# First token block of a hybrid decoder layer: scaling after the projections, and identity transposes on TensorE

## The chip, the cores and the metric

One core of a Trainium2 chip runs the whole layer in one program. The metric is the device time in microseconds of one execution. A profiled execution gives the trace that the rows below are read from.

## What is computed

A decoder layer on 2048 tokens of width 1024: a mixer (a gated linear recurrence beside a convolution module), attention into 256 fixed memory tokens, a convolutional gated feed-forward part, a last normalization. The change touches the first normalization and the projections that follow it:

```python
h = rms_norm(x, mix_norm_g)              # x * rsqrt(mean(x*x) + eps) * g, per token
z = h @ w_in                             # 1024 -> 2048
lru_x, lru_gate, conf_a, conf_b = jnp.split(z, [512, 1024, 1536], axis=-1)
lru_x = causal_dwconv(lru_x, lru_conv_w) + lru_conv_b
y_lru = rg_lru(lru_x, ...) * gelu(lru_gate)
c = causal_dwconv(conf_a * sigmoid(conf_b), conf_conv_w) + conf_conv_b
```

The factor rsqrt(mean(x*x) + eps) belongs to a token, so that multiplying a token by it before `h @ w_in` or the token's results after it is the same thing.

## The kernel before

**Order of the work.** The body of the program doesn't issue instructions. Generators (`mixer`, `memory_a`, `normed`, `attend`, `memory_vo`, `feed_forward` and others) append operations to a list, each stepping when a running count of TensorE work reaches its due time; of the due ones the first in the list `tasks` steps. A planner (`Program.schedule`) then plays all operations through with estimated costs, and so fixes the order in which each engine, and SP's queue of loads and stores, gets them. It ranks ready operations by due times derived from TensorE's order, except those appended while `pr.first` is set: they are ranked by their place in the list, ahead of all others. Buffers of a kind (84 of class S with 512 columns, 4 of class W for raw weights, 3 of class D for convolution inputs, 8 banks `ps`) are granted in the order in which the list asks for them. On the chip each engine keeps its planned order and waits on semaphores. Because every operation is emitted by the planner, the profile puts them all at L393; the names of the tiles tell them apart.

**Precision.** Operands are split into a rounded high part and the rest (`split`: a copy on ACT, a subtraction on VectorE; `split_scaled` does it with a factor for each channel). A product is three matmuls (`mm3`) of 128 by 128 against 128 by 512.

**Query block 0.** Tokens come in four blocks of 512, `q` = 0 to 3. `mixer(0)` starts with `first_norm` (from line 1055 of before): it loads the 8 tiles of x, then the first two raw blocks of w_in (`W_in.fetch`, columns 1536 to 1791, rows 0 to 511 and 512 to 1023), sums squares on ACT, turns the tokens on TensorE (8 times 4 transposes of 128 by 128) and multiplies by the gains, gets the token factors (square root, reciprocal), spreads them over all partitions by a matmul of `ones` and four diagonal matrices, multiplies the turned tokens by that row, splits them and multiplies: 8 steps `k` of 2 times 3 matmuls, 48 for one project of 256 columns. Before them `setup` has loaded the four gains (`v1024`), which TensorE turns as well.

**After it.** `conf` runs for c = 0 and 2: a project for the sigmoid (the first one is the one above), a project for its partner, product `cb`, 31 taps of convolution on VectorE (30 `scalar_tensor_tensor` a channel block into `conv`). `lru` runs for c = 0 and 2: project z, four taps that read the bank of z directly (`xc`), the last three columns of z kept in `ztail`, then gates, the recurrence, and a project with Gelu. In `memory_a`, beside it, the memory's keys and `w_q` are multiplied (tiles `kv`, `qt`, `mt`, `a`). Blocks q = 1 to 3 take `mix_norm` instead, which scales the tokens before it turns them. After a mixer, `normed` sums the convolutions (`sum`) for a layer norm, and `attend` goes on.

Of the kernel before, what the change touches and what calls it, by code (L numbers as in the profile page):

```python
# [14 lines left out]
ALU = mybir.AluOpType  # L15
# [19 lines left out]
LK = 4  # L35
# [381 lines left out]
def hybrid_layer(  # L417
# [336 lines left out]
    W_in = Columns(w_in[0], "w_in2", 16, NQ)  # L754
    W_out = Rows(w_out[0], "w_out2", 8, NQ)

    def conf(X, C, pb):
        for c in (0, 2):
            if pb is None:
                pb = yield from project(W_in, 3 * DL + c * P, X)  # L760
            sg = []
            for j in range(2):
                t = tmp("sg")
                ACT(t[:], pb[j][:], AF.Sigmoid)
                sg.append(t)
            pb = None
            yield 0
            pa = yield from project(W_in, 2 * DL + c * P, X)
            cbs = []
            for j in range(2):  # L770
                cb = pr.new("D", (P, CK - 1 + TT), name="cb")
                V("tensor_copy", cb[:, : CK - 1], ctail[c + j][:])
                V("tensor_tensor", cb[:, CK - 1 :], pa[j][:], sg[j][:], op=ALU.mult)
                V("tensor_copy", ctail[c + j][:], cb[:, TT : TT + CK - 1])
                cbs.append(cb)
            for j in range(2):
                a, cb, w = tmp("conv"), cbs[j], vec["v512"][:, c + j, :]
# [19 lines left out]

    def conf_out(C, Y):
        s = block_sum(C, False)
        yield 2  # L800
        p = ps()
        matmul(p[:], ones[:], s[:], start=True, stop=True)
        for c in range(NC4):
            V("tensor_tensor", C[c][:], C[c][:], p[:], op=ALU.subtract)
        ss = block_sum(C, True)
        yield 6
        r = wide_rstd(ss, 1.0)
        for c in range(NC4):
            w = vec["v512"][:, c, :]
            V("scalar_tensor_tensor", C[c][:], C[c][:], w[:, I_LG : I_LG + 1], r[:], op0=ALU.mult, op1=ALU.mult)  # L810
            ACT(C[c][:], C[c][:], AF.Silu, bias=w[:, I_LB : I_LB + 1])
            hi, lo = pair("y")
            split(C[c][:], hi, lo)
            Y.append((hi, lo))

    def lru(X, L):
        for c in (0, 2):
            pz = yield from project(W_in, c * P, X)
            H = []
            for j in range(2):  # L820
                w = vec["v512"][:, c + j, :]
                zt = ztail[c + j]
                xc = tmp("xc")
                ACT(xc[:], pz[j][:], AF.Identity, scale=w[:, I_LCW + 3 : I_LCW + 4], bias=w[:, I_LCB : I_LCB + 1])
                for s in range(1, LK):
                    wt = w[:, I_LCW + 3 - s : I_LCW + 4 - s]
                    V("scalar_tensor_tensor", xc[:, s:], pz[j][:, : TT - s], wt, xc[:, s:], op0=ALU.mult, op1=ALU.add)
                    V("scalar_tensor_tensor", xc[:, :s], zt[:, LK - 1 - s :], wt, xc[:, :s], op0=ALU.mult, op1=ALU.add)
                V("tensor_copy", zt[:], pz[j][:, TT - LK + 1 :])
                H.append(xc)  # L830
            yield 5
            for j in range(2):
                w = vec["v512"][:, c + j, :]
                xc = H[j]
# [25 lines left out]
            pg = yield from project(W_in, DL + c * P, X)  # L860
            for j in range(2):
                ge = tmp("gelu")
                ACT(ge[:], pg[j][:], AF.Gelu_apprx_tanh)
                V("tensor_tensor", ge[:], H[j][:], ge[:], op=ALU.mult)
                hi, lo = pair("y")
                split(ge[:], hi, lo)
                L.append((hi, lo))
# [32 lines left out]
    def memory_a():  # L900
# [30 lines left out]
        yield 2  # L931
        def operands(h):
            kk = yield from kv(h * M)
            yield 0
# [36 lines left out]

    def memory_vo():
        yield mem_a
        for h in range(4):
            vh, vl = yield from kv(D + h * M)
            yield 1
# [65 lines left out]
    def mixer(q, after):  # L1042
        if after:
            yield after
        if q == 0:
            X, pb = yield from first_norm()
        else:
            X, pb = (yield from mix_norm(q)), None
        C, L = [], []
        yield from conf(X, C, pb)  # L1050
        yield from lru(X, L)
        del X
        mixed[q] = C, L

    def first_norm():


        pr.first = True
        warm = small(1)
        ACT(warm[:], eps[:], AF.Sqrt)  # L1060
        xs = [[None, None] for _ in range(NTB)]
        st, T = Stats(), []
        for half in range(2):
            for tb in range(NTB):
                t = xs[tb][half] = tmp("x")
                pr.dma(t[:], x[0, tb * P : (tb + 1) * P, half * TT : (half + 1) * TT])
        raw = [W_in.fetch(3 * DL, kq) for kq in range(2)]
        for half in range(2):
            for tb in range(NTB):
                st.add(tb, half, xs[tb][half][:])  # L1070
            for k in range(half * KQ, (half + 1) * KQ):
                p = ps()
                with together():
                    for tb in range(NTB):
                        transpose(p[:, tb * P : (tb + 1) * P], xs[tb][half][:, (k % 4) * P : (k % 4 + 1) * P], ident[:])
                if not half:
                    t = tmp("xt")
                    V("tensor_scalar", t[:], p[:], vec["v1024"][:, k, G_MIX : G_MIX + 1], None, op0=ALU.mult)
                    p = t
                T.append(p)  # L1080
        del xs
        r = st.rstd()
        p, diag = ps(), []
        for tb in range(NTB):

            d = pr.new("S", (P, P), name="diag")
# [5 lines left out]
        ww = [W_in.rounded(3 * DL, 0, raw[0])]  # L1092
        X, pp = [], [ps(), ps()]
        for k, t in enumerate(T):
            if k < KQ:
                V("tensor_tensor", t[:], t[:], p[:], op=ALU.mult)
            else:
                if k == KQ:
                    row = tmp("row")
                    ACT(row[:], p[:], AF.Copy)  # L1100
                z, t = t, tmp("xt")
                V("scalar_tensor_tensor", t[:], z[:], vec["v1024"][:, k, G_MIX : G_MIX + 1], row[:], op0=ALU.mult, op1=ALU.mult)
            hi, lo = pair("x")
            split(t[:], hi, lo)
            X.append((hi, lo))
            if k == 1:
                ww.append(W_in.rounded(3 * DL, 1, raw[1]))
            kq, i = divmod(k, KQ)
            for f in range(2):
                wh, wl = ww[kq][f]  # L1110
                with together():
                    mm3(pp[f][:], wh[:, i, :], wl[:, i, :], hi[:], lo[:], k == 0, k == NK - 1)
        W_in.store(3 * DL, 0, ww[0])
        W_in.store(3 * DL, 1, ww[1])
        pr.first = False
        yield 0
        return X, pp

    def mix_norm(q):
        xs = load_x(q, "x")  # L1120
# [8 lines left out]
        yield 8  # L1129
        X = []  # L1130

        def take(k, p):
# [16 lines left out]
    def attend(q, ready):  # L1149
# [17 lines left out]
        yield 2  # L1167
        X = []

        def take(k, p):  # L1170
# [34 lines left out]
                row.append(t)  # L1205
            ys.append(row)
        del xs
        yield 6

        def take2(k, p):  # L1210
            t = tmp("xt")
# [341 lines left out]
        yield V_LATE  # L1553
        vec["v3072"] = columns([ffn_conv_w[0], ffn_conv_b], DFF, "v3072")

    EARLY, VO_WAIT, V_LATE = 5, 0, 500
    X = [HalfX(h) for h in range(NH)]

    def first_x():
        yield first_t  # L1560
        yield started[NQ - 1]
        for key in UP_ORDER[:EARLY]:
            X[0].make(key)
            yield 20

    def feed_forward():
        yield first
# [13 lines left out]
            tasks.insert(0, Task(finish(h, downs[h].acc)))  # L1581

    setup()
    mixers = [None] * NQ
    attends = [None] * NQ
    mixers[0] = spawn(mixer(0, None))
    spawn(setup_later(), mixers[0])
    mem_a = spawn(memory_a())
    mixers[1] = spawn(mixer(1, mixers[0]))
    normeds = [None] * NQ  # L1590
    normeds[0] = spawn(normed(0, [mixers[0]], 40))
    attends[0] = spawn(attend(0, [normeds[0]]))
    mem_vo = spawn(memory_vo())
    mixers[2] = spawn(mixer(2, mixers[1]))
    normeds[1] = spawn(normed(1, [attended[0]], 90), mixers[2])
    attends[1] = spawn(attend(1, [normeds[1]]))
    mixers[3] = spawn(mixer(3, mixers[2]))
    normeds[2] = spawn(normed(2, [attended[1]], 90), mixers[3])
    normeds[3] = spawn(normed(3, [mixers[3], normeds[2]], 55))
    attends[2] = spawn(attend(2, [normeds[2]]))  # L1600
    attends[3] = spawn(attend(3, [normeds[3], attended[2]]))
    first_t = spawn(X[0].kept(normeds[3], 10), attends[2])
    first = spawn(first_x(), attends[2])
    tail = spawn(feed_forward())
    drive()
    pr.emit(tc)

# [30 lines left out]
```

## Time and profile before

| | us |
|---|---|
| median of 3 runs | 2511.07 |
| lowest and highest | 2508.03, 2512.06 |
| profiled execution, device time | 2507.09 |
| its span, first to last instruction | 2505.3 |
| its mean granted TensorE clock | 0.996 |

Busy in the span: TensorE 2463.5 us, its weight loads 2037.9, VectorE 1820.2, ACT 1166.4, GpSimd 0.7. The DMA engines moved 543.68 MB, 217 GB/s on the mean.

In rows of the trace, PE is TensorE, PEld its weight loads, DVE VectorE, SPq the queue that issues transfers. A row of the view in order of time has the start, the time from the first start to the last end, the engine, the source line, the operation, `out<-in`, the shapes and the count; brackets hold the idle time just before it and what ended that. A row of the view by stretches has for each engine the busy time and, in brackets, the number of instructions, then the granted clock of TensorE (1.00 is 2.4 GHz, 0.50 is 1.2 GHz), the DMA engines' busy share and their GB/s.

### The profile page before, as it was taken

The page shows a single profiled execution, that of the slowest core. Times are in us where ns is not written, and L with a number is a line of the kernel's source. Part 1 is how long each engine was busy: PE and PEld are TensorE (multiplying, and loading weights), DVE is VectorE, ACT ScalarE, POOL GpSimd, SP SyncE. Part 2 cuts the span into 40 slices and gives each one's busy share as a digit, 9 for nine tenths or more (in the row PEclk, how much of TensorE's full clock was granted, in tenths as well). Part 3 has the DMA queues.
Part 4 walks back from the last instruction along what each step waited for, and adds up shares of the span by engine and source line. Part 5 has one row for each costly group of instructions (what it writes and reads, how often), then busy time and mean ns, then how long its engine had stood idle before and what let it go on. Part 6 is the DMA issues. An engine that isn't in the chain of part 4 may idle for free. (4 is left out here: it accounts for less than half of the span.)

```text
span 2505.3 us, 32662 instructions
## 1 busy us (share of the span) xinstructions
PE 2463.5 (98%) x11180; PEld 2037.9 (81%) x11180; DVE 1820.2 (73%) x3037; ACT 1166.4 (47%) x2034; POOL 0.7 (0%) x6
## 2 busy tenths in 40 slices
PE   8999999999999999999999999999999999999998
PEld 6798788887888788887888888788888888888887
DVE  7997985199429972339888887987866775667666
ACT  6472748335643564346454454654544432224223
POOL 0000000000000000000000000000000000000000
PEclk9999999999999999999999999999999999999999
DMA  8678585848553788558654545655422188779775
GB/s 308 201 236 303 172 298 192 319 163 288 199 213 124 249 290 311 201 178 281 232 178 171 176 150 191 238 178 172 148 72 97 64 279 286 255 242 338 259 252 177
DMA packets 327740, 543.68 MB, mean 217 GB/s; under 512 B 31580, under 2 KB 109404, under 8 KB 327574
## 3 DMA queue, kind: packets, MB, share of 16 engines
q1 hardware_dynamic: 327574, 541.60, 63.4%
q8 instruction: 88, 1.44, 0.2%
q14 instruction: 78, 0.64, 0.1%
HBM read 396.78 MB, written 144.70 MB: 216 GB/s over the span
## 5 line engine op out<-in xcount | busy, mean ns | idle before, releaser
L393 PE MATMUL ps<-Xh,wl 128*128 128x512 f32 x1344 | 523.6, 390 | 2.7 <-DVE wl L393 2.7
L393 PE MATMUL ps<-Xh,wh 128*128 128x512 f32 x1344 | 523.6, 390 | 1.8 <-ACT u L393 1.1
L393 PE MATMUL ps<-Xl,wh 128*128 128x512 f32 x1344 | 522.9, 389 | 0.0
L393 DVE SCALAR_TENSOR_TENSOR conv<-cb,v,conv 128x512 f32<-128x512 f32 x480 | 332.9, 745 | 2.4 <-ACT conv L393 2.1
L393 PEld LDWEIGHTS ps<-Xh,wl 128*128 128x128 f32 x1344 | 252.3, 188 | 57.8 <-DVE wl L393 5.3
L393 PEld LDWEIGHTS ps<-Xh,wh 128*128 128x128 f32 x1344 | 252.2, 188 | 55.9 <-ACT wh L393 1.9
L393 PEld LDWEIGHTS ps<-Xl,wh 128*128 128x128 f32 x1344 | 252.3, 188 | 52.1
L393 PE MATMUL ps<-wh,hidl 128*128 128x512 f32 x672 | 261.5, 389 | 0.4 <-DVE hidl L393 0.4
L393 PE MATMUL ps<-wh,hidh 128*128 128x512 f32 x672 | 261.5, 389 | 0.0
L393 PE MATMUL ps<-wl,hidh 128*128 128x512 f32 x672 | 261.4, 389 | 0.0
L393 DVE TENSOR_TENSOR acc<-acc,ps 128x512 f32<-128x512 f32 x192 | 129.6, 685 | 145.3 <-PE ps L393 142.8
L393 PE MATMUL ps<-xh,wh 128*128 128x512 f32 x512 | 203.5, 397 | 8.5 <-DVE ztail L393 6.2
L393 PE MATMUL ps<-xl,wh 128*128 128x512 f32 x512 | 202.2, 395 | 0.2 <-DVE xl L393 0.2
L393 PE MATMUL ps<-xh,wl 128*128 128x512 f32 x512 | 201.7, 394 | 0.0
L393 ACT ACTIVATE wh<-s 128x512 fp32r<-128x512 f32 x192 | 119.6, 628 | 134.0 <-DVE s L393 96.8
L393 DVE TENSOR_TENSOR wl<-raw,wh 128x512 fp32r<-128x512 f32 x208 | 140.9, 686 | 33.2 <-ACT wh L393 27.1
L393 DVE TENSOR_TENSOR wl<-s,wh 128x512 fp32r<-128x512 f32 x192 | 131.2, 686 | 46.0 <-ACT wh L393 30.3
L393 ACT ACTIVATE wh<-raw 128x512 fp32r<-128x512 f32 x208 | 127.2, 627 | 76.3 <-PE ps L393 42.2
L393 ACT ACTIVATE u<-ps 128x512 f32<-128x512 f32 x144 | 85.9, 597 | 144.7 <-PE ps L393 143.2
L393 PEld LDWEIGHTS ps<-wh,hidl 128*128 128x128 f32 x672 | 126.1, 188 | 27.1 <-DVE hidl L393 0.8
L393 PEld LDWEIGHTS ps<-wh,hidh 128*128 128x128 f32 x672 | 126.1, 188 | 26.5 <-ACT hidh L393 0.4
L393 PEld LDWEIGHTS ps<-wl,hidh 128*128 128x128 f32 x672 | 126.1, 188 | 26.1
(199 smaller groups left out, 4240.9 us busy)
## 6 DMA issues: line engine op xcount, KB each, us to landing
raw<-in_w_up_dram SPq DMA_DIRECT2D x96, 512.0 KB
wh<-w_down SPq DMA_DIRECT2D x164, 256.0 KB
wl<-w_down SPq DMA_DIRECT2D x164, 256.0 KB
wh<-w_in SPq DMA_DIRECT2D x96, 256.0 KB
wl<-w_in SPq DMA_DIRECT2D x96, 256.0 KB
hid<-cv SPq DMA_DIRECT2D x48, 512.0 KB
h<-hid SPq DMA_DIRECT2D x96, 256.0 KB
w_down<-wh SPq DMA_DIRECT2D x84, 256.0 KB
```

The costliest lines, as they stand in the source:

```text
L393: getattr(e, name)(*[resolve(a) for a in args], **{k: resolve(a) for k, a in kw.items()})
```

## The change

For block 0 alone, `first_tokens` takes the place of `first_norm`. The tokens are turned, multiplied by the gains and split without the token factor; the sums of squares, the factor and its row (`row`) come behind the first project in the list. Results of block 0's projects are multiplied by `row` on VectorE by a new helper `scaled`: ahead of the sigmoid and behind it (for its partner), on z into a tile in SBUF which the taps and `ztail` then read, and ahead of Gelu. The loads are put in another order: half of x, a block of w_in, half of x, a block of w_in. Two groups of 16 transposes of the identity into a bank that nobody reads (`kept_busy`) are put before the turning of the tokens and before the first matmul; `since` dates them for the planner. The second half of the tokens is turned between the matmuls of the first half. Blocks 1 to 3 have `row` None. Constants for waits and for the order of tasks get names, with the values that they had; three generators get a `yield 0` more.

```diff
+    def scaled(name, p, row):
+        if row is None:
+            return p
+        t = tmp(name)
+        V("tensor_tensor", t[:], p[:], row[:], op=ALU.mult)
+        return t
...
-    def conf(X, C, pb):
+    def conf(X, C, pb, row):
...
-                ACT(t[:], pb[j][:], AF.Sigmoid)
-                sg.append(t)
+                ACT(t[:], scaled("sg", pb[j], row)[:], AF.Sigmoid)
+                sg.append(scaled("sg", t, row))
...
-    def lru(X, L):
+    def lru(q, X, L, row):
...
-                xc = tmp("xc")
-                ACT(xc[:], pz[j][:], AF.Identity, scale=w[:, I_LCW + 3 : I_LCW + 4], bias=w[:, I_LCB : I_LCB + 1])
+                xc, z = tmp("xc"), scaled("z", pz[j], row)
+                ACT(xc[:], z[:], AF.Identity, scale=w[:, I_LCW + 3 : I_LCW + 4], bias=w[:, I_LCB : I_LCB + 1])
+                if q in Z_COPIED:
+                    z = tmp("z")
+                    ACT(z[:], pz[j][:], AF.Copy)
...
-                V("tensor_copy", zt[:], pz[j][:, TT - LK + 1 :])
+                V("tensor_copy", zt[:], z[:, TT - LK + 1 :])
...
-                ACT(ge[:], pg[j][:], AF.Gelu_apprx_tanh)
+                ACT(ge[:], scaled("gelu", pg[j], row)[:], AF.Gelu_apprx_tanh)
...
-    def first_norm():
+    def first_tokens():
...
+        def kept_busy(n, since):
+            p = ps()
+            with together():
+                for i in range(n):
+                    pr.do("PE", "transpose", p[:, :P], ident[:], ident[:], reads=[since])
+
+        kept_busy(16, vec["v1024"])
         for half in range(2):
             for tb in range(NTB):
                 t = xs[tb][half] = tmp("x")
                 pr.dma(t[:], x[0, tb * P : (tb + 1) * P, half * TT : (half + 1) * TT])
-        raw = [W_in.fetch(3 * DL, kq) for kq in range(2)]
...
+            raw.append(W_in.fetch(3 * DL, half))
+        X, pp, ww = [], [ps(), ps()], []
+
+        def turn(k):
+            half = k // KQ
+            p = ps()
+            with together():
+                for tb in range(NTB):
+                    transpose(p[:, tb * P : (tb + 1) * P], xs[tb][half][:, (k % KQ) * P : (k % KQ + 1) * P], ident[:])
+            hi, lo = pair("x")
+            split_scaled(p[:], vec["v1024"][:, k, G_MIX : G_MIX + 1], hi[:], lo[:])
+            X.append((hi, lo))
+            if k in (0, KQ + 1):
+                ww.append(W_in.rounded(3 * DL, half, raw[half]))
+
+        for k in range(KQ):
+            turn(k)
+        kept_busy(16, xs[NTB - 1][0])
+        for k in range(NK):
+            half = k // KQ
+            hi, lo = X[k]
+            for f in range(2):
+                wh, wl = ww[half][f]
+                with together():
+                    mm3(pp[f][:], wh[:, k % KQ, :], wl[:, k % KQ, :], hi[:], lo[:], k == 0, k == NK - 1)
+            for i in ((), (KQ,), (KQ + 1,), (KQ + 2, KQ + 3))[k] if not half else ():
+                turn(i)
+        st = Stats()
...
-            if k < KQ:
-                V("tensor_tensor", t[:], t[:], p[:], op=ALU.mult)
...
-                V("scalar_tensor_tensor", t[:], z[:], vec["v1024"][:, k, G_MIX : G_MIX + 1], row[:], op0=ALU.mult, op1=ALU.mult)
-            hi, lo = pair("x")
-            split(t[:], hi, lo)
...
+        ACT(row[:], p[:], AF.Copy)
...
-        return X, pp
+        return X, pp, row
...
+    EARLY, VO_WAIT, V_LATE, Z_COPIED = 5, 0, 500, ()
+    MIX_WAIT, MIX_TURN, LN_SUM, LN_SQ, GATES = (0, 0, 0, 0), 8, 2, 6, 5
```

## Rows read from the trace of the kernel before

**Rows 1.** The page's first part: busy time of the engines, share, instructions.
```profile
PE 2463.5 (98%) x11180; PEld 2037.9 (81%) x11180; DVE 1820.2 (73%) x3037; ACT 1166.4 (47%) x2034; POOL 0.7 (0%) x6
```

**Rows 2.** View by stretches; columns named in its first line.
```profile
core 0: us, PE busy (x) PEld busy (x) DVE busy (x) ACT busy (x) POOL busy (x), PEclk, DMA share, GB/s
0.00:10.00 10.00, 4.74 (x22) 3.81 (x23) 3.32 (x15) 4.73 (x11) 0.70 (x6) 1.00 0.68 208
10.00:20.00 10.00, 6.43 (x36) 5.00 (x35) 7.44 (x16) 6.19 (x15) 0.00 (x0) 0.93 0.48 144
20.00:30.00 10.00, 7.67 (x20) 5.23 (x20) 6.54 (x12) 6.83 (x14) 0.00 (x0) 0.56 0.99 316
...
100.00:150.00 50.00, 47.41 (x245) 40.69 (x245) 49.67 (x86) 34.68 (x54) 0.00 (x0) 1.00 0.39 125
```

**Rows 3.** TensorE in order of time, 3 to 30 us; columns in its first line.
```profile
start us, us, engine line op out<-in xcount [idle before <-releaser]
3.33 0.98 PE L393 MATMUL ps<-ident,raw 4*128 4x4 f32 x8 [3.33 <-DMA raw<-in_ffn_norm_g_dram]
7.67 1.54 PE L393 MATMUL ps<-ident,x 128*128 128x128 f32 x6 [0.18 <-DMA x<-in_x_dram]
...
11.65 1.68 PE L393 MATMUL ps<-ident,x 128*128 128x128 f32 x13 [0.21 <-DMA x<-in_x_dram]
...
17.58 0.41 PE L393 MATMUL ps<-ident,raw 42*128 42x42 f32 x4 [2.54 <-DMA raw<-in_conf_ln_b_dram]
...
23.48 0.79 PE L393 MATMUL ps<-xh,wh 128*128 128x512 f32 x1 [2.33 <-ACT xh L393]
...
28.97 0.40 PE L393 MATMUL ps<-xh,wh 128*128 128x512 f32 x1
29.20 0.39 PE L393 MATMUL ps<-xl,wh 128*128 128x512 f32 x1
```

**Rows 4.** ACT in order of time, 14 to 36 us.
```profile
14.44 1.15 ACT L393 ACTIVATE wh<-raw 128x512 fp32r<-128x512 f32 x2 [0.18 <-DMA raw<-in_w_in_dram]
...
22.28 0.63 ACT L393 ACTIVATE wh<-raw 128x512 fp32r<-128x512 f32 x1 [4.83 <-DMA raw<-in_w_in_dram]
...
30.25 0.63 ACT L393 ACTIVATE wh<-raw 128x512 fp32r<-128x512 f32 x1
...
35.79 0.60 ACT L393 ACTIVATE sg<-ps 128x512 f32<-128x512 f32 x1
```

**Rows 5.** SP's queue in order of time: the load of w_in's third block.
```profile
17.76 0.56 SPq L393 DMA_DIRECT2D raw<-in_w_in_dram x1
```

**Rows 6.** TensorE in order of time, 81 to 122 us.
```profile
81.19 3.61 PE L393 MATMUL ps<-mt,raw 128*128 128x256 f32 x16
88.38 0.77 PE L393 MATMUL ps<-xh,wh 128*128 128x512 f32 x1 [3.57 <-DVE ztail L393]
...
93.64 0.43 PE L393 MATMUL ps<-xh,gwah 128*128 128x512 f32 x1
...
121.67 0.47 PE L393 MATMUL ps<-xh,wh 128*128 128x512 f32 x1 [2.59 <-DVE ztail L393]
```

**Rows 7.** VectorE in order of time: ztail at 88 us, then 201 to 222 us.
```profile
88.09 0.14 DVE L393 COPY ztail<-ps 128x3 f32<-128x3 f32 x1
...
201.47 0.74 DVE L393 SCALAR_TENSOR_TENSOR conv<-cb,v,conv 128x512 f32<-128x512 f32 x1
...
210.43 0.69 DVE L393 TENSOR_TENSOR sum<-conv 128x512 f32<-128x512 f32 x1 [8.00 <-PE ps L393]
...
213.59 1.29 DVE L393 TENSOR_TENSOR wl<-raw,wh 128x512 fp32r<-128x512 f32 x2 [1.01 <-ACT wh L393]
218.59 0.69 DVE L393 TENSOR_TENSOR cb<-ps,sg 128x512 f32<-128x512 f32 x1 [3.71 <-PE ps L393]
...
220.22 1.54 DVE L393 SCALAR_TENSOR_TENSOR conv<-cb,v,conv 128x512 f32<-128x512 f32 x2 [0.72 <-ACT conv L393]
```

**Rows 8.** TensorE's waits, 200 to 300 us: total, times, longest.
```profile
PE ps L393 <- ACT xh L393: 3.1, 1, 3.1
```

More of the change, by code (lines that the diff above doesn't have):

```diff
@@ L799, in conf_out @@
         s = block_sum(C, False)
-        yield 2
+        yield LN_SUM
         p = ps()
@@ L805, in conf_out @@
         ss = block_sum(C, True)
-        yield 6
+        yield LN_SQ
         r = wide_rstd(ss, 1.0)
@@ L822, in lru @@
                 zt = ztail[c + j]
-                xc = tmp("xc")
-                ACT(xc[:], pz[j][:], AF.Identity, scale=w[:, I_LCW + 3 : I_LCW + 4], bias=w[:, I_LCB : I_LCB + 1])
+                xc, z = tmp("xc"), scaled("z", pz[j], row)
[3 more added lines that the diff above has]
+                    ACT(z[:], pz[j][:], AF.Copy)
                 for s in range(1, LK):
                     wt = w[:, I_LCW + 3 - s : I_LCW + 4 - s]
-                    V("scalar_tensor_tensor", xc[:, s:], pz[j][:, : TT - s], wt, xc[:, s:], op0=ALU.mult, op1=ALU.add)
+                    V("scalar_tensor_tensor", xc[:, s:], z[:, : TT - s], wt, xc[:, s:], op0=ALU.mult, op1=ALU.add)
                     V("scalar_tensor_tensor", xc[:, :s], zt[:, LK - 1 - s :], wt, xc[:, :s], op0=ALU.mult, op1=ALU.add)
-                V("tensor_copy", zt[:], pz[j][:, TT - LK + 1 :])
+                V("tensor_copy", zt[:], z[:, TT - LK + 1 :])
                 H.append(xc)
-            yield 5
+            yield GATES
             for j in range(2):
@@ L930, in memory_a @@
         pr.first = False
-        yield 2
+        yield MEM_WAIT
         def operands(h):
@@ L973, in memory_vo @@
         yield mem_a
+        yield VO_LATE
         for h in range(4):
@@ L1044, in mixer @@
             yield after
+            yield MIX_WAIT[q]
         if q == 0:
-            X, pb = yield from first_norm()
+            X, pb, row = yield from first_tokens()
         else:
-            X, pb = (yield from mix_norm(q)), None
+            X, pb, row = (yield from mix_norm(q)), None, None
         C, L = [], []
-        yield from conf(X, C, pb)
-        yield from lru(X, L)
-        del X
+        yield from conf(X, C, pb, row)
+        yield from lru(q, X, L, row)
+        del X, row
         mixed[q] = C, L
-    def first_norm():
+    def first_tokens():
         pr.first = True
@@ L1061, in first_norm @@
         xs = [[None, None] for _ in range(NTB)]
-        st, T = Stats(), []
+        raw = []
+        def kept_busy(n, since):
[4 more added lines that the diff above has]
+        kept_busy(16, vec["v1024"])
         for half in range(2):
@@ L1066, in first_norm @@
                 pr.dma(t[:], x[0, tb * P : (tb + 1) * P, half * TT : (half + 1) * TT])
-        raw = [W_in.fetch(3 * DL, kq) for kq in range(2)]
-        for half in range(2):
-            for tb in range(NTB):
-                st.add(tb, half, xs[tb][half][:])
[L1071 to L1080, printed above, removed]
+            raw.append(W_in.fetch(3 * DL, half))
[24 more added lines that the diff above has]
+        st = Stats()
+        for tb in range(NTB):
+            for half in range(2):
+                st.add(tb, half, xs[tb][half][:])
         del xs
         r = st.rstd()
-        p, diag = ps(), []
+        p, diag, row = ps(), [], tmp("row")
         for tb in range(NTB):
@@ L1091, in first_norm @@
                 matmul(p[:, tb * P : (tb + 1) * P], ones[:], diag[tb][:], start=True, stop=True)
-        ww = [W_in.rounded(3 * DL, 0, raw[0])]
-        X, pp = [], [ps(), ps()]
-        for k, t in enumerate(T):
-            if k < KQ:
-                V("tensor_tensor", t[:], t[:], p[:], op=ALU.mult)
[L1097 to L1101, printed above, removed]
-                V("scalar_tensor_tensor", t[:], z[:], vec["v1024"][:, k, G_MIX : G_MIX + 1], row[:], op0=ALU.mult, op1=ALU.mult)
-            hi, lo = pair("x")
-            split(t[:], hi, lo)
[L1105 to L1112, printed above, removed]
+        ACT(row[:], p[:], AF.Copy)
         W_in.store(3 * DL, 0, ww[0])
@@ L1128, in mix_norm @@
                 ACT(xs[tb][half][:], xs[tb][half][:], AF.Copy, scale=r[:, tb : tb + 1])
-        yield 8
+        yield MIX_TURN
         X = []
@@ L1166, in attend @@
         V("tensor_scalar", rn[:], r[:], -(M ** -0.5), None, op0=ALU.mult)
-        yield 2
+        yield ATT_TURN
         X = []
@@ L1207, in attend @@
         del xs
-        yield 6
+        yield FFN_TURN
         def take2(k, p):
@@ L1554, in setup_later @@
         vec["v3072"] = columns([ffn_conv_w[0], ffn_conv_b], DFF, "v3072")
-    EARLY, VO_WAIT, V_LATE = 5, 0, 500
+    EARLY, VO_WAIT, V_LATE, Z_COPIED = 5, 0, 500, ()
+    MIX_WAIT, MIX_TURN, LN_SUM, LN_SQ, GATES = (0, 0, 0, 0), 8, 2, 6, 5
+    MEM_WAIT, VO_LATE, ATT_TURN, FFN_TURN, X_PACE, T_PACE = 2, 0, 2, 6, 20, 10
+    NORMED = [lambda: ([m[0]], 40), lambda: ([attended[0]], 90), lambda: ([attended[1]], 90), lambda: ([m[3], n[2]], 55)]
+    ATTEND = [lambda: [n[0]], lambda: [n[1]], lambda: [n[2]], lambda: [n[3], attended[2]]]
+    TURNS = lambda: [later, m[0], mem_a, m[1], n[0], a[0], mem_vo, n[1], m[2], a[1], n[2], m[3], n[3], first_t, first, a[2], a[3], tail]
     X = [HalfX(h) for h in range(NH)]
@@ L1563, in first_x @@
             X[0].make(key)
-            yield 20
+            yield X_PACE
     def feed_forward():
@@ L1583, in hybrid_layer @@
     setup()
[L1584 to L1604, printed above, removed]
+    mixers, normeds, attends = ([Task(None) for _ in range(NQ)] for _ in range(3))
+    later, mem_a, mem_vo, first_t, first, tail = (Task(None) for _ in range(6))
+    m, n, a = mixers, normeds, attends
+    for q in range(NQ):
+        m[q].gen = mixer(q, m[q - 1] if q else None)
+        n[q].gen = normed(q, *NORMED[q]())
+        a[q].gen = attend(q, ATTEND[q]())
+    later.gen, mem_a.gen, mem_vo.gen = setup_later(), memory_a(), memory_vo()
+    first_t.gen, first.gen, tail.gen = X[0].kept(n[3], T_PACE), first_x(), feed_forward()
+    tasks.extend(TURNS())
     drive()
```

## Prediction

> **What bounds the kernel now.** I read the page's engine table first: TensorE is busy 2463.5 of 2505.3 us [rows 1]. Its work can hardly shrink here, so a change to the first tokens can only win back time in which TensorE stands still or runs at half clock. The view by stretches says where that is [rows 2]: in the first 10 us TensorE is busy 4.74, in the second 6.43, in the third 7.67 and that at a mean clock of 0.56; from 100 to 150 us it loses 2.6 more, and there VectorE is busy 49.67 of 50.
>
> The order of TensorE's instructions gives the causes [rows 3]. The first 32 transposes go as the tokens land. The 0.22 us between starts in the row at 7.67 ((1.54-0.42)/5, one instruction lasting 0.42) is half rate, 0.12 us at 11.65 ((1.68-0.27)/12, one lasting 0.27) full rate, so the clock rose at about 11.6. (The clock column reads 1.00 for the first 10 us all the same [rows 2]; ahead of the first change that it sees, I trust the spacing.) Then the multiplication needs normalized tokens: TensorE has idled up to 17.58, multiplies a little, and idles again to 23.48 on ACT's xh. Why ACT was late is in its own row [rows 4]: the rounding of the third block of w_in stands ahead of the next xh and waits 4.83 us for its load. That load was issued at 17.76 [rows 5]. After such pauses the clock is at the lower of its two levels, 1.2 GHz: of the next matmuls a dozen took 5.5 us, from 23.48 to 28.97, and then it is one in 0.23 [rows 3]. The 48 matmuls of the first projection end where ACT reads their sum, 35.8 [rows 4].
>
> Then TensorE is full until 84.8, waits 3.57 us for VectorE's last read of a bank (the copy to ztail), runs 12 matmuls at half clock, and near 119 waits 2.59 us for the same copy [rows 6]. VectorE, full of convolution, is done with query block 0 at 202.2, and then is idle for 8.00, 1.01, 3.71 and 0.72 us, 13.4 in all, until TensorE brings block 1 [rows 7].
>
> **The front.** Removed from the way to the first matmul: eight squares on ACT, the root and reciprocal, the diagonals, their product and twelve VectorE passes over the tokens. What gates it now is the first half of x, the first block of w_in and its rounding.
> - x: the four first tiles still lead the queue; the last of them lands at 7.67 [rows 3].
> - Identity: 16 instructions need only the identity matrix on the chip, though the planner dates them by v1024. They follow the eight small transposes, which end at 4.3 (3.33+0.98), at 0.22 each: to 7.8, when x is there. Cover: an otherwise idle TensorE, cost at most 0.2.
> - Clock: it rose after the back-to-back transposes from 7.67 to 11.6, 3.9 us; back to back from 4.3, about 8.2. So 16 real transposes at 0.12 end near 10, and the second 16 identities near 12.
> - Weights: the first block has half the bytes of those four tiles, which took 3.3 to 7.7, so by half of that time my estimate is landing near 9.9. ACT and VectorE round it in 0.63+0.69, 11.2: hidden by the identities. The second half of x and the second block have come when ACT stops waiting for it at 14.44 [rows 4], as before, since the queue holds the same bytes; they are wanted at about 17.
> - Products: from 12 on, 48 at 0.23 are 11.0 and 16 transposes 1.9, to 24.9. The row's four products, two instructions each, and four small transposes for v512 add 12 at 0.12, 1.4: the next project can start at 26.3. Before, it started when the sum was out at 35.8, so I take 35.6. Gain 9.3. The squares, now behind, fit beside the products on ACT.
> - Loads: the queue order ahead of the third block stays (eight tokens, two blocks, small columns, gates), so I leave it at landing 22.28. Rounded near 23.6, it is in time for 26.3. The fourth is rounded from 30.25 on [rows 4], ready near 31.6, and wanted 24 matmuls, 5.5 us, after 26.3: at 31.8. It is only just covered; I take 0.3 for it, front gain **9.0**; bounds 3 (the old ACT block returns) and 11.
>
> **The unscaled results.** VectorE gets 16 more multiplications in block 0: eight at sigmoid, four at z, four at gelu. The like of it took 0.69 at 218.59, and two in a row 1.29 at 213.59 [rows 7], so 0.60 more for each that follows: I use 0.61, 9.8 us. The four at z do something more: they are the only readers of TensorE's bank, where before the bank waited for seven interleaved reads, the last the copy at 88.09 [rows 7]. A bank is free about 1 us after its project ends. So the pause of 3.57, its 12 matmuls at half clock (93.64-88.38 = 5.26 against 12 x 0.23 = 2.76, so 2.5) and the pause of 2.59 should go: **8.7** us, bounds 0 and 8.7. Next late there is the input of the gates: they went at 93.64, 12.4 after the end of z at 81.19, and TensorE has 14.6 us of other work for that time (16 instructions of kv in 3.61, a project in 11.0), if its weights are rounded.
>
> **What VectorE gives back.** Its work on block 0 ends 9.0 earlier and 9.8 later, at about 203.0. TensorE would be 17.7 earlier, and the slack between the two was 13.4: VectorE is short by 17.7+0.8-13.4 = 5.1 us when block 1 arrives. Convolution yields to urgent work and is only summed there, so the price lies between 0 and 5.1. The nearest row is the one pause that TensorE makes in the full stretch 200 to 300, 3.1 us on ACT's xh [rows 8]; I charge one more of it, **+3.1**. The order written out anew (task list, constants) has the old values, and an extra wait of zero gives the turn to the same task: 0, no cover needed.
>
> Sum: -9.0 - 8.7 + 3.1 = -14.6 against the profiled execution's 2507.1, so 2492.5. The median of the runs shown, 2511.1, is 4.0 above that execution; as a median I say **2496.5**.
>
> **A rule against it.** The row at 11.65 shows transposes reaching full rate after nothing but transposes. The Trainium skill (TensorE: Matmul & The Clock Gate, Part 4: PE-mode transpose) says that full clock does not engage for transposes, as they don't count as busy in the same way. By that rule the identities would warm nothing; this case's trace speaks against it, 0.22 us falling to 0.12. What it would do here is worked out from rows as rival 1: 2502 where the trace's way gives 2496.5.
>
> **Rivals.**
> 1. Turning the identity does not hold the clock, so the change doesn't do what it says. Transposes at 0.22 move the first matmul to about 15; the next dozen lose what those from 23.48 to 28.97 lost, 5.5 - 12 x 0.23 = 2.7: 5.7 of the front is gone. -3.3-8.7+3.1: 2498.2 profiled, 2502 median. The 0.56 of the third stretch, which follows idling, and the row at 11.65 speak against. 0.07.
> 2. The bank pauses come back as another wait: z's multiplication queues behind convolution, or the gates' chain is late because VectorE is full. Only the front stays: -9.0, 2498.1, median 2502. For: 49.67 of 50 us. Against: the one multiplication needs only one turn among convolutions of about 0.7 each. 0.18.
> 3. The third block's rounding stands ahead of the last xh on ACT again: the products resume at 23.5 as before, on fewer matmuls (24, not 42), gain 3, and the bank pauses are replaced as in 2: 2504, median 2508. For: the load lands at 22.28, whatever the planner thinks. Against: the xh should be made before 19. 0.11.
> 4. Slower: VectorE sets the pace of block 0. TensorE would follow it through the buffers for the convolution and the banks, so the stage ends when VectorE ends: start gained less 9.8. It decides for slower by over 5 us where the front gives under 4.8; with rival 3's front of 3 it is +6.8: 2513.9, median 2518. For: VectorE is full from 100 to 150. Against: it idles 13.4 after 202.2, and the pause near 119 is all that TensorE loses there (2.59 of 2.6). 0.09.
>
> **How the numbers follow.** The forecast has 0.55, the rivals 0.07, 0.18, 0.11 and 0.09. A measurement here tells about 0.2%, 5.0 us, from no change; faster means below 2506. Forecast, 1 and 2 lie there: 0.80; rival 3 is within: 0.11; rival 4 slower: 0.09. The forecast's own ends are front 11 with no price from VectorE, 2491, and front 7 with 5.1 paid, 2500.5. Rival 3 must be in and rival 4 can stay out; below 2491 I add 4 us, the spread of the runs shown: 2487 to 2509.
>
> **What would show it.** Front: matmuls with xh from about 12, spaced 0.23 at once, no TensorE pause above 1 us to 26, sigmoid near 27. Half spacing there would be rival 1; a pause on ACT xh before a raw load, rival 3. Banks: no wait on ztail in block 0; in its place a wait on xh or on z would be rival 2. VectorE: idle about 203 short or gone, TensorE's 3.1 us pause on xh in block 1 longer by a like amount. I would be wrong by more than the range if loads after the third block starve TensorE between 26 and 60 us, which the fourth block's 30.25 leaves only just covered, or if the planner's new order brings new pauses after 300 us, which nothing here calls for.

## The result, and the profile after

| us | before | after |
|---|---|---|
| median | 2510.18 (6 runs) | 2497.06 (6 runs) |
| lowest to highest | 2508.03 to 2512.16 | 2494.59 to 2499.72 |
| profiled execution: time, span | 2507.09, 2505.3 | 2498.48, 2496.7 |

After / before is 0.9948, 95% interval 0.9935 to 0.9961: 13.1 us less on the medians. The forecast median was 2496.5. The two profiled executions differ by 8.6 only, since that of before is a quick one and that of after a slow one; what is known of the other 4.5 us is told with the point on the total.

The view by stretches of the kernel after, columns as in [rows 2]:

```profile
0.00:10.00 10.00, 6.59 (x39) 6.60 (x40) 2.10 (x13) 3.32 (x6) 0.70 (x6) 1.00 0.63 202
10.00:20.00 10.00, 10.00 (x63) 8.71 (x62) 6.24 (x10) 8.54 (x21) 0.00 (x0) 1.00 0.41 140
20.00:30.00 10.00, 7.71 (x31) 5.87 (x30) 5.57 (x14) 5.29 (x11) 0.00 (x0) 0.83 1.02 348
...
100.00:150.00 50.00, 50.00 (x288) 44.33 (x287) 49.73 (x89) 39.18 (x63) 0.00 (x0) 1.00 0.59 191
...
200.00:300.00 100.00, 94.02 (x398) 76.20 (x397) 98.68 (x171) 46.80 (x67) 0.00 (x0) 0.97 0.62 218
```

The last of these stretches in the kernel before, same view:

```profile
200.00:300.00 100.00, 96.17 (x416) 78.93 (x415) 86.19 (x152) 38.84 (x57) 0.00 (x0) 0.98 0.64 223
```

TensorE is full from 10 to 20 and from 100 to 150 us, where it lost 3.6 and 2.6 before [rows 2]. From 200 to 300 it loses 2.2 more than before, and VectorE, which had 13.8 us to spare there, has 1.3.

TensorE after, in order of time (compare [rows 3]):

```profile
4.32 3.67 PE L393 MATMUL ps<-ident 128*128 128x128 f32 x16
7.79 2.50 PE L393 MATMUL ps<-ident,x 128*128 128x128 f32 x16
10.12 1.91 PE L393 MATMUL ps<-ident 128*128 128x128 f32 x16
11.79 0.48 PE L393 MATMUL ps<-xh,wh 128*128 128x512 f32 x1
...
24.03 0.50 PE L393 MATMUL ps<-xh,wh 128*128 128x512 f32 x1 [1.99 <-ACT xh L393]
...
26.14 0.63 PE L393 MATMUL ps<-xh,wh 128*128 128x512 f32 x1
26.56 0.63 PE L393 MATMUL ps<-xl,wh 128*128 128x512 f32 x1
...
28.70 1.42 PE L393 MATMUL ps<-diag,ones 128*128 128x128 f32 x8
29.88 0.48 PE L393 MATMUL ps<-xh,wh 128*128 128x512 f32 x1
```

The first matmul is at 11.79 (12 was forecast). The identities before the tokens go at 0.22 us each, those after at 0.11, so the clock came up between. But the seventh step of the first project waits 1.99 us for its xh and then falls to half rate (0.42 from 26.14 to 26.56), so that the next project begins at 29.88 and not at 26.3. What ACT did is in its row:

```profile
22.77 0.63 ACT L393 ACTIVATE wh<-raw 128x512 fp32r<-128x512 f32 x1 [4.13 <-DMA raw<-in_w_in_dram]
23.31 1.25 ACT L393 ACTIVATE xh<-ps,v 128x512 fp32r<-128x512 f32 x2
```

It is the row of 22.28 [rows 4] again: the rounding of w_in's third block stands ahead of the last two xh and waits 4.13 us for its load. How much this costs differs between executions: in e13, the same kernel, the next project begins at 29.30.

The banks of z after, VectorE in order of time (compare [rows 7]):

```profile
74.43 0.68 DVE L393 TENSOR_TENSOR z<-ps,row 128x512 f32<-128x512 f32 x1
76.29 0.68 DVE L393 TENSOR_TENSOR z<-ps,row 128x512 f32<-128x512 f32 x1
```

TensorE after, in order of time, around them and in block 1 (compare [rows 6]):

```profile
75.92 3.61 PE L393 MATMUL ps<-mt,raw 128*128 128x256 f32 x16
87.54 0.39 PE L393 MATMUL ps<-xh,gwah 128*128 128x512 f32 x1
...
247.83 0.74 PE L393 MATMUL ps<-xh,gwah 128*128 128x512 f32 x1 [4.43 <-ACT xh L393]
```

z's project ends at 75.92, 5.3 us earlier than before (81.19 [rows 6]), and its second bank is read out by 77.0. TensorE doesn't stop before the gates at 87.54; the two pauses of [rows 6] are gone. The pause in block 1 [rows 8] has grown from 3.13 to 4.43.

How far TensorE is ahead can be read off one instruction in both kernels, from the view of one tile (the last two numbers before the shapes are the start of the first and of the last one). Before:

```profile
L393 PE MATMUL ps<-kvh,qth x64: 282/283/364, 145.7 to 185.8; 128*128 128x256 f32 x64
L393 PE MATMUL ps<-wh,yh x256: 387/389/799, 309.0 to 1019.8; 128*128 128x512 f32 x128
```

The same view after:

```profile
L393 PE MATMUL ps<-kvh,qth x64: 283/283/467, 131.5 to 171.6; 128*128 128x256 f32 x64
L393 PE MATMUL ps<-wh,yh x256: 387/389/1415, 298.2 to 1011.2; 128*128 128x512 f32 x128
```

14.2 us ahead at 145.7 and still at 185.8; 10.8 at 309.0; 8.6 at 1019.8, and it stays 8.6. The same rows for all runs, with the lead over the one profile of before:

| run | lead at 145.7 | at 185.8 | at 309.0 | at 1019.8 | median, us | ratio, 95% interval |
|---|---|---|---|---|---|---|
| after | 14.2 | 14.2 | 10.8 | 8.6 | 2497.1 | 0.9948 (0.9935 to 0.9961) |
| e13, after again | 14.7 | 14.8 | 11.4 | 10.6 | 2497.4 | 0.9947 (0.9934 to 0.9959) |
| e1, no turning | 13.6 | 13.7 | 10.9 | 10.2 | 2497.1 | 0.9943 (0.9925 to 0.9961) |
| e2, bank held | 3.8 | 3.9 | 2.6 | 0.5 | 2507.0 | 0.9983 (0.9974 to 0.9993) |
| e3, before with z copied | 10.1 | 10.2 | 9.3 | 8.3 | 2501.2 | 0.9958 (0.9945 to 0.9972) |
| e8, twelve left out | 12.5 | 12.6 | 11.7 | 11.1 | 2496.7 | 0.9952 (0.9938 to 0.9967) |
| e11, e3 and early block | 11.2 | 11.2 | 10.2 | 9.2 | 2499.0 | 0.9956 (0.9939 to 0.9973) |
| e4, early block | 16.9 | 17.0 | 14.0 | 13.2 | 2493.2 | 0.9930 (0.9914 to 0.9945) |
| e14, e4 again | 18.0 | 18.1 | 15.4 | 15.1 | 2493.4 | 0.9931 (0.9918 to 0.9945) |
| e7, early, no turning | 16.9 | 16.9 | 13.5 | 11.2 | 2495.2 | 0.9945 (0.9930 to 0.9960) |
| e9, early, z of block 1 copied | 18.0 | 18.0 | 15.1 | 14.7 | 2494.1 | 0.9941 (0.9926 to 0.9956) |
| e10, early, z of blocks 1 to 3 | 18.1 | 18.1 | 14.0 | 9.3 | 2496.3 | 0.9949 (0.9932 to 0.9966) |
| e12, early, GpSimd | 16.0 | 16.0 | 12.4 | 11.7 | 2495.2 | 0.9940 (0.9925 to 0.9955) |

Each profile is one execution; e4 and e14 are one program and differ by 1.1 us at the first mark. So 1 us in a lead says nothing. Three us is more than any two profiles of one program differ by at the first three marks; at the last, two executions of the change differ by 2.0.

### The profile page after: what moved, and what is told of

Read it like the earlier page. It is cut to its first block, busy times and chain, and to the rows that moved or that the text cites. A ratio compares the mean times of both kernels' runs of the same rounds, so it can differ in the third digit from the quotient of the medians.

```text
span 2496.7 us, 32736 instructions
## 1 busy us (share of the span) xinstructions
PE 2466.2 (99%) x11212; PEld 2042.8 (82%) x11212; DVE 1821.8 (73%) x3041; ACT 1172.3 (47%) x2039; POOL 0.7 (0%) x6
```

## The experiments

The theory after the result: the front gives 5.7 us because ACT's wait takes back 3.6 of the forecast 9.3, the bank of z gives 8.5, VectorE's lack of time takes 3.4 between 186 and 309 us. Rivals: turning the identity is what the front gains; the pauses on ztail went for another reason; the pause in block 1 hangs on banks.

**e1: without the identities.**

```diff
-        kept_busy(16, vec["v1024"])
-        kept_busy(16, xs[NTB - 1][0])
```


> The changed kernel without both groups of identity transposes; all else as in the change. Theory of the clock: TensorE then starts at 7.7 us on the real transposes at half rate (0.22 us each, 16 of them to 11.3), the clock comes up near 11.6 as in the kernel before, or later if the first matmuls find it low: between 0 and 12 matmuls at 0.43 instead of 0.23, so 0 to 2.4 us later at the 24th matmul. But TensorE has 2 us to spare before the seventh xh (24.0 us), so the next project would start 0 to 1 us later than its 29.9 and the time be 2497 to 2498. Rival, that the turning is where the front gain comes from: 3 to 5 us slower than the change, about 2501. Rival, that transposes do nothing to the clock: the same spacings as with the turning, 2497, and the first matmul no later than 11.8.

TensorE of e1 in order of time:

```profile
7.98 3.03 PE L393 MATMUL ps<-ident,x 128*128 128x128 f32 x13 [0.68 <-DMA x<-in_x_dram]
10.84 0.79 PE L393 MATMUL ps<-xh,wh 128*128 128x512 f32 x1
11.43 0.49 PE L393 MATMUL ps<-xl,wh 128*128 128x512 f32 x1
11.77 0.40 PE L393 MATMUL ps<-xh,wl 128*128 128x512 f32 x1
...
24.71 0.51 PE L393 MATMUL ps<-xh,wh 128*128 128x512 f32 x1 [3.21 <-ACT xh L393]
```

The time is that of the change, 2497.1. Without identities in its way the first matmul is 0.95 earlier, and after two slow matmuls the clock is up, from the 13 real transposes. TensorE then only waits longer for xh, 3.21 in place of 1.99. The next project starts at 30.43, against 29.88 and 29.30 in the two profiles of the change. In this kernel the turning has no measurable effect on the time.

**e2: the change, with the bank of z held to the end of the taps.**

```diff
-                V("tensor_copy", zt[:], z[:, TT - LK + 1 :])
+                V("tensor_tensor", zt[:], pz[j][:, TT - LK + 1 :], row[:, TT - LK + 1 :], op=ALU.mult)
```


> The changed kernel, with z's last three columns for ztail read from TensorE's bank (times the row) in place of from the copy in SBUF: as much work, the same front, but the bank is held to the end of the taps again. Theory, that the single reader of z's bank removed the two pauses: waits on ztail of about 3.6 and 2.6 us come back in block 0 near 80 and 112 us, with some matmuls at half clock after the first; TensorE is then 5.7 and not 14.2 us ahead of the kernel before at the first kvh matmuls, and the time about 2497+8.7-3 = 2503. Rival, that the pauses went because TensorE and VectorE meet otherwise after a shorter front: no wait on ztail over 1 us, 2497.

TensorE of e2 in order of time:

```profile
74.21 3.61 PE L393 MATMUL ps<-mt,raw 128*128 128x256 f32 x16
...
82.77 0.77 PE L393 MATMUL ps<-xh,wh 128*128 128x512 f32 x1 [4.95 <-DVE ztail L393]
...
116.51 0.76 PE L393 MATMUL ps<-xh,wh 128*128 128x512 f32 x1 [2.76 <-DVE ztail L393]
```

One read of three columns, moved from SBUF to the bank, brings both pauses back, the first longer than before, and the time to 2507.0. So it is the single reader of the bank that removed them; the rival falls. What is left of the change without it is about 4 us; with the 9.7 us that e3, the next run, finds for the bank alone, that is 13.7, about the whole change. The run is 4 us slower than expected. Its z ends 7.0 us ahead of the kernel before (74.21 against 81.19), but at 145.7 only 3.8 are left: its pauses are 1.5 us longer in sum, and half rate follows both of them, where [rows 6] has full rate after the second.

**e3: the kernel before, with z of block 0 copied.**

```diff
+                xc, z = tmp("xc"), pz[j]
+                if q == 0:
+                    z = tmp("z")
+                    V("tensor_copy", z[:], pz[j][:])
```


> The kernel before, with z of block 0 copied by VectorE into SBUF and the taps and ztail reading that copy: the bank part of the change alone, with 4 more VectorE passes (2.4 us), and the old front. Theory: the ztail pauses near 85 and 119 us go, 6.1 + 2.6 = 8.7 us ahead at the first kvh matmuls; VectorE's slack of 13.4 us before block 1 covers 8.7 + 2.4, so little is paid back: 2510 - 8.7 + 0 to 2 = 2502 to 2504. Rival, that the pauses change their name only: 2508 to 2511.

TensorE of e3 goes from z's end to the gates without a pause, as after:

```profile
80.22 3.61 PE L393 MATMUL ps<-mt,raw 128*128 128x256 f32 x16
91.85 0.39 PE L393 MATMUL ps<-xh,gwah 128*128 128x512 f32 x1
```

2501.2: four copies in the kernel before are worth some 9 us, with the tokens still scaled first. Of the 10.1 us lead 1.0 is there already when z ends (80.22 against 81.19), in a front that no edit touched, and so lies between executions; the other 9.1 are the pauses and the half rate, 8.7 by [rows 6].

**e4, e14: the change, with the third block loaded early.**

```diff
             raw.append(W_in.fetch(3 * DL, half))
+        W_in.early[2 * DL, 0] = W_in.fetch(2 * DL, 0)
...
+            st = self.early.pop(key, None)
+            n = self.seen[key] = 1 if st else self.seen.get(key, 0) + 1
...
+            got = self.rounded(c0, kq, st or self.fetch(c0, kq))
```


> The changed kernel, with the load of w_in's third block put right behind the second one, ahead of the small columns and gates. Theory, that ACT's wait of 4.13 us for this block held back the last two xh: the block lands near 16.5 instead of 22.7 us, no pause of TensorE before the end of the first project, full clock there, the next project starts near 26.2 instead of 29.9 and the lead of 3.7 us stays, less what VectorE lacks then: 2494 to 2496. Rival, that the loads are what limits this stage: TensorE pauses for the fourth block instead, at about 31 us, and the time is 2497; rival, that VectorE paces block 0: lead lost by 300 us, 2497.

ACT of e4 in order of time:

```profile
18.61 0.62 ACT L393 ACTIVATE wh<-raw 128x512 fp32r<-128x512 f32 x1
19.13 1.25 ACT L393 ACTIVATE xh<-ps,v 128x512 fp32r<-128x512 f32 x2
```

TensorE of e4 in order of time:

```profile
24.31 1.05 PE L393 MATMUL ps<-diag,ones 128*128 128x128 f32 x8
25.12 0.48 PE L393 MATMUL ps<-xh,wh 128*128 128x512 f32 x1
```

The same start in e14:

```profile
26.07 0.48 PE L393 MATMUL ps<-xh,wh 128*128 128x512 f32 x1
```

The third block's rounding goes at 18.61 without a wait, the xh follow, and the next project starts at 25.12 (26.07 in e14) in place of 29.88. Of these 4.8 us 2.7 are left in the lead at 145.7: TensorE's waits between have 0.9 us on sg and 0.7 on mem, which the change doesn't have. In e14, without these two, 3.8 are left of 3.8. The time falls to 2493.2: the wait on ACT was what the front lacked. It is the quickest kernel of the study. It ran once more beside the change on one chip (as did the change, for a question below):

> The third block loaded early, once more beside the changed kernel. Theory: 3 to 5 us faster than that, 2492 to 2494, with the next project starting near 25.1 us and a lead of 16.9 us at the first kvh matmuls again. Rival, that the difference was the chip's: within 1.5 us of the changed kernel.

2492.74 to 2495.02 in five runs against 2496.77 to 2499.33: the two don't overlap, and the medians are 4.0 us apart.

**e7: the early block without the identities.** The edits of e1 on e4.

> The third block loaded early, and both groups of identity transposes taken out: whether turning the identity is worth anything once ACT no longer holds up the last xh. Theory from the run without turning: the 16 real transposes alone bring the clock up near 11.4 us, the first matmul starts near 10.9 instead of 11.5 us with two matmuls at most at half rate, so the next project starts at 24.5 to 25.1 us and the time is 2492 to 2494, that of the early block with turning. Rival, that the gain of turning was only hidden by ACT's wait: the next project starts 2 to 3 us later than 25.1 and the time is 2496.

TensorE of e7 in order of time:

```profile
11.74 0.63 PE L393 MATMUL ps<-xl,wh 128*128 128x512 f32 x1
12.17 0.63 PE L393 MATMUL ps<-xh,wl 128*128 128x512 f32 x1
...
13.31 0.39 PE L393 MATMUL ps<-xh,wl 128*128 128x512 f32 x1
...
25.74 0.48 PE L393 MATMUL ps<-xh,wh 128*128 128x512 f32 x1
```

The first four matmuls are at half rate, and the next project starts 0.62 us later than in e4, but earlier than in e14, which turns the identity. The median is 1.9 above that of e4, but the intervals overlap and the leads at the first marks are equal. So a gain by the turning isn't shown here either.

**e8: 12 of the 16 multiplications left out.** The calls of `scaled` at the sigmoid and at Gelu replaced by their operands.

> The changed kernel with 12 of the 16 multiplications by the row left out (those at the sigmoid and at Gelu, so that block 0's gates get unscaled values and the output is another one); z is still multiplied. 7.3 us less for VectorE in block 0. Theory, that VectorE's lack of time takes back 3.4 us of the lead of 14.2 between 172 and 310 us: the pause on xh in block 1 falls from 4.4 to 3.1 us and the other small ones go, the lead at 310 us is 13 to 14 and the time 2494. Rival, that the pause on xh hangs on the order of the work and the banks in block 1 and not on VectorE's load: the pause stays at 4.4 us and the time at 2497.

TensorE's waits up to 320 us in e8 (total, times, longest):

```profile
PE ps L393 <- ACT xh L393: 5.5, 2, 3.1
PE ps L393 <- DVE xc L393: 1.7, 1, 1.7
```

The pause in block 1 is back at 3.1, and between 186 and 309 us only 0.9 of the lead is lost, against 3.4 in both profiles of the change. VectorE is busy 14.8 us from 200 to 220 us, 19.9 in the change and 6.7 before. So with time to spare on VectorE most of the loss is gone. But it doesn't follow VectorE's load step by step: e4 and e14, up to 3.8 us further ahead with the same load, lose 3.0 and 2.7, no more than the change, and e12 below, with four multiplications less on VectorE, loses 3.6. The time of e8, 2496.7, is no better than the change's: in the order that the planner made for this kernel TensorE waits 1.7 us on xc in block 0, which the change does not. What sixteen multiplications cost in all is not shown.

**e9, e10: early block, and z of later blocks copied by ACT.** `Z_COPIED = (1,)`, then `(1, 2, 3)`.

> The third block loaded early, and in query block 1 z copied to SBUF by ACT for the taps (the constant Z_COPIED set to block 1). Theory, that block 1's pause of 4.4 us on xh and the half clock behind it come from the banks of z as in block 0, so that TensorE has nothing else to do until the gates: it goes, and the time is 2493 - 4 to 6 = 2487 to 2489. Rival, that VectorE is late with the taps whatever the banks do: the pause stays or moves, 2492 to 2494.

> As the run before it, for query blocks 1 to 3. Theory of the banks: blocks 2 and 3 lose little on them (the pauses of TensorE between 500 and 900 us are on sum, yh and wl, each under 3 us), so within 2 us of the run with block 1 alone: 2486 to 2490. Rival, that four more copies on ACT in each block delay the roundings there: 2492 to 2496.

The longest wait of e9 up to 320 us:

```profile
PE ps L393 <- ACT xh L393: 4.5, 1, 4.5
```

The pause in block 1 is not moved by a bank that is free early, so the bank theory falls there: what cured block 0 does nothing in block 1. ACT's two copies are done by 239.2, and TensorE stands from 239.9 to 244.4 all the same, for the gates' xh, whose taps VectorE finishes among its convolutions. With three blocks copied the lead drops from 14.0 at 309 to 9.3 at 1019.8 us and the time is 2496.3, worse than e4. TensorE waits there 1.3 us for ACT's xh at 817, which e9 doesn't. This points at the rival, ACT's extra copies, but accounts for a part of the loss only.

**e11: e3 with the early block**, that is the bank part and the load order without the unscaled tokens.

> The kernel before, tokens scaled first as there, with z of block 0 copied to SBUF and the load of w_in's third block right behind the second: the bank part and the load order without the unscaled tokens and without turning. Theory, that ACT's wait for the third block was the larger part of the old front's loss: matmuls go on from 17.9 us at the pace of VectorE's 1.3 us for each of 8 steps, the next project starts near 30 us in place of 35.6, the lead at the first kvh matmuls is about 14 us, as the change has, and the time is 2496 to 2498. Rival, that the unscaled tokens are what shortens the front: the next project still starts at 33 us or later and the time is near the 2501 of the bank part alone.

TensorE of e11 in order of time:

```profile
19.86 0.62 PE L393 MATMUL ps<-ident,raw 42*128 42x42 f32 x4 [4.89 <-DMA raw<-in_conf_ln_b_dram]
20.41 0.80 PE L393 MATMUL ps<-xh,wh 128*128 128x512 f32 x1
...
33.81 0.39 PE L393 MATMUL ps<-xh,wh 128*128 128x512 f32 x1
```

2499.0, between the two expectations. ACT has the third block in time now, but the small columns come after it, and TensorE, which has their transposes ahead of its first matmul, waits 4.89 us for them; the first matmul is at 20.41. The old front moves the wait from one queue to another, so this run doesn't price the load order by itself. It does show that the load order doesn't make the front short without the unscaled tokens: the next project, the 49th matmul, starts at 33.81 there, as the rival said, against 34.85 in e3, 35.79 before and 29.88 in the change.

**e12: the early block, with four multiplications on GpSimd.**

```diff
-                sg.append(scaled("sg", t, row))
+                    u = tmp("sg")
+                    pr.do("Pool", "tensor_tensor", u[:], t[:], row[:], op=ALU.mult)
+                    sg.append(u)
```


> The third block loaded early, and the four multiplications of the sigmoid's result by the row put on GpSimd in place of VectorE: 2.4 us less for VectorE in block 0. Theory of VectorE's lack of time: the pause on xh in block 1 shrinks from 4.4 towards 3.1 us and the time is 1 to 2 us under the 2493 of the early block alone: 2491 to 2492. Rival, from the run with twelve multiplications left out, which was no faster in all: 2493. Rival, that GpSimd's slower pass holds up the products cb, or slows VectorE beside it: 2494 to 2497.

GpSimd of e12, in order of time:

```profile
31.65 3.07 POOL L393 TENSOR_TENSOR sg<-sg,row 128x512 f32<-128x512 f32 x2 [30.35 <-ACT sg L393]
51.05 2.07 POOL L393 TENSOR_TENSOR sg<-sg,row 128x512 f32<-128x512 f32 x1 [16.33 <-ACT sg L393]
```

These take 1.3 to 2.1 us each by the trace, and VectorE 0.69. The time is 2495.2, not under e4, and the pause in block 1 is 4.1. So the run settles nothing about VectorE's load, and there is no gain.

**e13: the change once more.**

> The changed kernel itself, to be compared with the early block on one chip, and for a second profile. In its first profile 2.2 us of the lead went between 310 and 890 us, where the same pauses as in the kernel before (2.6 us on sum, 2.5 on yh) were followed by a lower clock (0.93 in 800 to 850 us against 1.00). Theory, that after a pause of this length the clock falls in some executions and not in others of one program: this profile may show 1.00 there, lead at 890 us then 10 to 11 us; time 2497. Rival, that the changed kernel's own order of work brings the clock down: 0.93 again and a lead of 8.6 us.

The view by stretches for TensorE alone (busy, instructions, clock, DMA share, GB/s), the first profile of the change:

```profile
800.00:850.00 50.00, 47.03 (x189) 0.93 0.73 259
```

The same stretch of e13:

```profile
800.00:850.00 50.00, 46.53 (x199) 1.00 0.74 263
```

In both profiles TensorE waits there for yh for 2.5 us. In one the clock falls after it, in the other it doesn't, and that one loses only 0.8 of its lead from 309 to 1019.8 us, the first 2.2. It is one program, so the changed order of work is not the cause of that difference.

## Why the prediction was right, point by point

- **Total: right, 2496.5 against 2497.06**, and the likeliest case is the one that came. The front was off by 3.3 us and the other two terms by 0.2 and 0.3, all to the same side: against the profiled span the measured sum is -5.7 - 8.5 + 3.4 = -10.8 at 309 us and -8.6 in the end, where -14.6 was forecast, and the profiled execution took 2498.48 and not 2492.5. The medians are further apart than the two profiles, by 4.5 us, and that makes up for it: the agreement to 0.6 us is luck to this extent. The profiled execution of before was quicker than all its six listed runs (2507.09 against 2508.03 to 2512.16), that of after is above its median, and e13's span, of the same kernel, is 1.1 us shorter. The mean granted clock goes with this: in 37 further executions of before, beside the experiments, it is 0.991 to 0.998, with a median of 0.993 (0.996 in the profile), in the 11 of the change 0.995 to 0.998, with a median of 0.997. At a clock of 0.995 before takes 2508.7 on the mean and the change 2498.5, 10.2 less. So some 3 us of the 13.1 go with a lower clock in most executions of before; where in the kernel it falls in these, no trace shows. The prediction carried the 4.0 us between profile and median over from before to the change, whose median is 1.4 below its profile.
- **The front: step mis-sized, 9.0 forecast, 5.7 measured** (6.3 in e13). x, the identities and the weights were right to 0.3 us (first matmul 11.79). The step that failed is that rival 3 was put aside with "the xh should be made before 19": the planner did put the third block's rounding ahead of the last two xh, with the load landing at 22.77. The rival was given as one case with the bank pauses coming back; it came by itself, in a smaller form (12 matmuls left, not 24). e4 shows it: with the block early the next project starts at 25.12 (26.07 in e14), even under the 26.3 worked out. The sigmoid, expected near 27, goes at 32.07, behind the row at 30.16.
- **The banks: right.** 8.7 forecast; 14.2 - 5.7 = 8.5 found. e2 and e3 show the cause from both sides, by taking it out of the change and putting it into the kernel before. (A bank of z had five readers, one of ACT and four of VectorE; the prediction's seven counts three operations on ztail that don't read it.)
- **VectorE: right in size, 3.1 charged and 3.4 lost.** The mechanism is shown in part: the slack after block 0 was used up (86.19 to 98.68 busy), and in e8, with slack left, the loss is 0.9. The sum behind it, 17.7 + 0.8 - 13.4, makes VectorE shorter of time the further TensorE is ahead; e4 and e14 don't bear out that the loss grows with that. That it would show as one more pause of 3.1 was not so: the pause itself grew by 1.3, the half rate behind it cost 1.3 more, and the rest is small.
- **The identities: the cost was nothing, but so was the gain.** The forecast counted on them for full clock at 12 us. The trace has it; e1 and e7 have it too, from the real transposes, within 1.2 us. That the clock does come up on transposes was right: from 4.3 to 11.8 us TensorE does nothing but transposes, and they fall from 0.22 to 0.11 us each. This is against the rule of the Trainium skill (TensorE: Matmul & The Clock Gate, Part 4: PE-mode transpose) that full clock does not engage for transposes. But rival 1 had asked the wrong question: the real transposes are enough.
- **The loads behind the third block**, named as the main danger, did not starve TensorE: no such wait stands in the list between 30 and 180 us.

## What to carry to other kernels

Ask for each TensorE bank who reads it last: one copy to SBUF ahead of several reads was worth 9 us here by itself, at 2.4 us of a full VectorE, and the place can be found in the list of waits, by a small copy that a matmul waits for. A load that is needed later can hold up what is needed now, if its first user stands ahead of the urgent work in an engine's fixed order; look at the row that waits for DMA, and at what stands behind it. A lead won at one place can be lost again at another: compare the start of one instruction in both traces at several marks to see where it goes. A median that comes out as forecast doesn't show that the terms did: here the front was a third short.

## What the runs showed of the hardware

- After a pause of TensorE of 2.46 us the clock fell in one of two executions of one program and stayed at 2.4 GHz in the other (0.93 and 1.00 in the same 50 us). The length of the pause alone doesn't tell: after 1.99 us, to 24.03 in the change, the clock is at 1.2 GHz from 26.1 on; after 2.59 us, to 121.67 in the kernel before, matmuls go at 0.23 us; after 2.76 us, to 116.51 in e2, at 0.43. Between the two profiles of the change this goes with 1.4 us from 309 to 1019.8 us.
- The granted clock column reads 1.00 in the first 10 us of all these profiles, while the transposes from 4.32 us on in the change take 0.22 us each, twice what they take from 10 us on. The spacing of like instructions tells the level there, the column doesn't.
- GpSimd took 1.3 to 2.1 us for a product of two 128x512 tiles in SBUF (e12) that VectorE does in 0.69.
